# Emptying both banks of a matmul pair first: one change to a two-layer diffusion trunk on one core

## The chip, the cores and the metric

The kernel runs on one core of one Trainium2 chip. The metric is the device time of one execution in microseconds (us). The core has five engines with a queue each: TensorE (PE, with its weight loads as PEld), VectorE (DVE), ScalarE (ACT), GpSimd (POOL) and SyncE (SP), which issues nearly all DMAs. Each queue is worked off in order.

## The reference

One inference step of a backbone with two layers over 128 context tokens and 512 latent tokens, width 2048, float32. T is 640, the tokens of both groups together.

```python
for l in range(DEPTH):                                   # DEPTH = 2
    shift, scale, gate = modulation(c, ada_w[l], ada_b[l])    # c_ctx for the context tokens
    h = rms_norm(x, norm_g[l]) * (1.0 + scale) + shift
    if l % 2 == 0:   # windowed attention || gated linear attention
        y, side = even_mixer(h, w_in_even, ...)          # (concat of both) * silu(gate columns)
    else:            # neighbourhood attention || chunked spatial-gating MLP
        y, side = odd_mixer(h, w_in_odd, ...)            # (concat of both) * silu(gate columns)
    x = x + gate * (y @ w_out[l])
y = rms_norm(x, final_norm_g)
```

Nearly all the work is the products with `w_in_even`, `w_in_odd` and `w_out`. The products are taken at float32 accuracy from three float32r products (high x high, high x low, low x high).

## The kernel before

**Layout.** Activations lie feature-major: 16 k-tiles of 128 features x 640 tokens, split into a high and a low part (`acth`, `actl`, in the code `ah`, `al`). Two columns ahead of the tokens carry the modulation's shift, so that the projection of the shift comes out of the same matmuls. A chunk is 128 output features; it fills two PSUM banks of 320 tokens each (`pa`, `pb`). Weights are loaded to `wraw` or `rs`, ACT copies the high part to `whi`, and POOL or DVE subtracts it to leave the low part, `wlo`.

**Chunks and pairs.** Single chunks run in `chunk`, most of both output projections and of layer 1 in `spair`, a Strassen-like product over two chunks that uses folded sums of k-tiles (`eh`, `el`). Where one projection ends and the next begins, two chunks run together in `kpair`, k-tile by k-tile: a pair that frees k-tiles one by one is followed by a pair that takes the rewritten ones one by one. `STEPS` and `LAST` are the orders of the k-tiles, `skew` lets the second chunk lag the first by two steps. There are three such junctions: layer 0's last two gate chunks before the first output projection; that projection's last two chunks before layer 1's first v chunks; layer 1's last two gate chunks before the second output projection. `handover` starts the tasks of a junction: `loader` brings k-tiles from DRAM into free slots, `rewrite` (ACT and DVE or POOL) splits them into `acth` and `actl` as the old ones come free and raises `y0:k`, `x1:k` or `y1:k`, and two `fold` tasks build the folded sums, spill the second halves of six k-tiles to DRAM (`bh_dram`, `bl_dram`) and then refold them in place.

**Evacuation.** When a chunk is done its closure `evac(pa, pb)` is called. For a gate chunk (`gate`) it multiplies each half by `rstd`, adds the shift's projection (`bc`) inside a Silu, and multiplies the result `g` into y, half after half. For an output chunk (`out_evac`) it computes `x + G * psum`, squares it and adds the square to `ssq`, half after half; the x tile was loaded by the chunk's `pre`, called at the pair's start. `rstd1` turns `ssq` into layer 1's `rstd`.

**Order.** The emitted order of all instructions is fixed ahead by a planner written in the kernel: `Pace` keeps a model time for each engine and each range of a tile; `self.now` is PE's. Between matmuls `tick` advances the tasks in the list `self.tasks`, in order of the list, and the weight splits (`wpump`). A task yields a delay or waits for flags (`wait`), for data (`until`) or for an engine's queue to be short (`calm`); `need` lets the plan's time pass until a flag is up. Every vector, scalar and GpSimd instruction carries line 214, the matmuls of the projections 397, every SP load 431; groups are told apart by their tiles.

Of the kernel before, what the change touches and what calls it, by code (L numbers as in the profile page):

```python
# [239 lines left out]
class Trunk:  # L240
# [122 lines left out]
    def arena(self, slots):  # L363

        pool = self.tc.tile_pool(name=f"ar{self.n}", bufs=1)
        self.n += 1
        self.ar_pool = pool
        p = pool.__enter__()
        self.ar = self.t(p, [128, int(slots * T)], "arena")
        self.ar_at = 0  # L370
# [423 lines left out]
    def kpair(self, c1, c2, order, ready=None, free=None):  # L794

        for c in (c1, c2):
            if self.chunks[c][3]:
                self.chunks[c][3]()
        banks = {}
        self.quiet = True  # L800
        steps = self.skew(c1, c2, order)
        for i, (c, k) in enumerate(steps):
# [12 lines left out]
            if k == order[-1]:  # L815
                self.chunks[c][4](*banks[c])
                self.drop(*banks[c])
                self.flags.add(f"evac{c}")
        self.quiet = False

    def hpair(self, c1, c2, after):
# [150 lines left out]
    def handover(self, ready, free, used, order, at, src, loads, spare, cs, shift=None):  # L972
# [68 lines left out]
        def fold(w):  # L1041
# [30 lines left out]
            for i in range(w, NS, 2):  # L1072
                j, m = pairs[i]
                yield from self.wait(f"{used}:{j}")
                h, l = (x[:, j, CW:] for x in (self.ah, self.al))
                nc.vector.tensor_tensor(q, f32(self.ah[:, m, CW:]), f32(self.al[:, m, CW:]), ALU.add)
                sub(q, q, f32(h))
                sub(q, q, f32(l))
                yield from split(h, l, q)
                yield  # L1080
# [69 lines left out]
    def gate(self, y, ring):  # L1150
        nc = self.nc
        box = {}

        def evac(pa, pb):
            if pa is not None:
                bc = box["bc"] = self.s("bc", 2)
# [44 lines left out]

    def ssq_add(self, ssq, x, k, sq, c=slice(0, T), eng=None):
        nc = self.nc
        if k == 0:
            nc.scalar.activation(ssq[:, c], x[:, c], AF.Square)
        else:
            sq = sq[:, : c.stop - c.start]
            nc.scalar.activation(sq, x[:, c], AF.Square)
            (eng or nc.gpsimd).tensor_tensor(ssq[:, c], ssq[:, c], sq, ALU.add)

# [720 lines left out]
    def out_evac(self, l, n, f, xsrc, spill):  # L1931
# [3 lines left out]
        def square(y, c):  # L1935
            if l == 1 and f == KT - 1:
                nc.scalar.activation(self.sq[:, : c.stop - c.start], y[:, c], AF.Square)
            else:
                eng = nc.vector if l == 0 and n >= KT - 2 else nc.gpsimd
                self.ssq_add(self.ssq, y, f, self.sq if self.cut == CUT else self.sqs.next(), c, eng)  # L1940

        def evac(pa, pb):
            G, at = self.G[l], self.cut
            y = self.Y[:, n % NY, :]
            if pa is not None:
# [8 lines left out]
                )  # L1954
                square(y, slice(0, at))
            if pb is not None:
# [3 lines left out]
                )  # L1960
                square(y, slice(at, T))
                if l == 0 or n < NY:
                    self.dma(spill[:, f, :], y)

        def pre():
# [148 lines left out]
    def program(self):  # L2114
# [121 lines left out]
        def gate_chunk(w, y, pre=(), ring="gz", begin=None, then=None):  # L2236
            box = {}

            def evac(pa, pb):
                if "f" not in box:  # L2240
                    self.need(*pre)
                    box["f"] = self.gate(y() if callable(y) else y, L[ring])
                box["f"](pa, pb)
                if pb is not None and then:
                    then()

            add(w, 128, True, begin, evac)


        def open_att():  # L2250
            self.need("gla_done3")
            self.rp.__exit__(None, None, None)
            self.close_arena()
            self.arena(18.5)
            L["hq"], L["gx"] = self.take(T, 3), self.take(T, 2)
            L["hk"] = Ring([Y[:, 6, :], self.take()])
# [158 lines left out]

        do(lambda: self.spawn(rstd1(co)))
        do(lambda: self.spawn(last_gate()))
# [4 lines left out]
        for ct in range(8):  # L2422
# [11 lines left out]
            pre = (f"gv{ct - 4}",) if ct > 3 else ("r10", "r11")  # L2434
            add(wO[32 + ct], 128, True, None, lazy("vr", pre=pre, then=vdone, slots="DER"))
            if ct == 1:
# [363 lines left out]
```

## Time and profile before

| what | value |
|---|---|
| median of 3 runs | 2108.09 us (2107.87 to 2108.88) |
| profiled execution, its own time | 2113.52 us |
| its span | 2111.7 us |
| mean granted TensorE clock | 0.994 |
| PE, DVE, ACT, POOL busy | 2056.5, 1304.9, 1079.9, 1297.6 us |

The span is that of one profiled execution, 5.4 us over the median with what lies around it. In the views a row of a timeline has its start, its length, engine, line, operation, `out<-in` by the program's tile names, shapes and count; the bracket tells the idle time before it on that engine and what ended it. The row of a window has the stretch, its length, the busy time of PE, PEld, DVE, ACT and POOL with counts, the granted clock, the DMA engines' share and GB/s. `arena` holds working tiles (the slots A to E and R, gate products, x tiles), `adas` three more slots, `Y` the mixer's output.

The junctions lie, in that span, at about 820 to 895, 1035 to 1095 and 1850 to 1905 us.

### The profile page before, as it was taken

To read this page: it belongs to the slowest core of one execution; us is meant where nothing else is said; L and a number is where in the kernel's file an instruction comes from. 1 tells how busy PE (TensorE), PEld (TensorE's weight loads), DVE (VectorE), ACT (ScalarE), POOL (GpSimd) and SP (SyncE) were. 2 spreads that over 40 slices of the span, in tenths; PEclk is the share of its full clock that TensorE was granted. 3 is DMA by queue.
4 is the path that set the end of the run, shared out by engine and by line. 5 is a ranking of instruction groups with operands and counts; after the bars stand their busy time and mean duration, and the time that the engine had idled before them with its cause. 6 is when DMAs were issued, how large, how long until landed. Compare 5 with 4: busy or idle time off the path is not lost. (4 is left out here: it accounts for less than half of the span.)

```text
span 2111.7 us, 40271 instructions
## 1 busy us (share of the span) xinstructions
PE 2056.5 (97%) x14345; PEld 2004.6 (95%) x14345; DVE 1304.9 (62%) x3034; ACT 1079.9 (51%) x2493; POOL 1297.6 (61%) x1090
## 2 busy tenths in 40 slices
PE   7999999999999999999999999999999999999997
PEld 6899999999999999999989999999999999999996
DVE  4746686676465664797376878787454544455334
ACT  5645565454566766544564444444444554454443
POOL 4656565355455554798654666655555577768884
PEclk9999999999999999999999999999999999999999
DMA  9966343335465544575633455444222344363426
GB/s 355 391 210 213 117 135 130 117 115 174 148 204 173 173 159 148 164 228 181 228 121 107 137 160 149 138 156 144 94 82 94 97 140 131 116 223 120 137 93 239
DMA packets 192840, 340.17 MB, mean 161 GB/s; under 512 B 20896, under 2 KB 70144, under 8 KB 192640
## 3 DMA queue, kind: packets, MB, share of 16 engines
q1 hardware_dynamic: 191296, 336.45, 48.4%
q8 instruction: 112, 1.84, 0.4%
q10 hardware_dynamic: 1344, 1.17, 0.2%
q14 instruction: 88, 0.72, 0.1%
HBM read 303.03 MB, written 31.88 MB: 159 GB/s over the span
## 5 line engine op out<-in xcount | busy, mean ns | idle before, releaser
L397 PE MATMUL bank<-acth,whi 128*128 128x320 f32 (+3 forms) x3320 | 1023.2, 319 | 14.5 <-ACT bc L214 4.5
L397 PE MATMUL bank<-actl,whi 128*128 128x320 f32 (+3 forms) x3320 | 994.9, 311 | 2.6 <-POOL actl L214 1.4
L397 PE MATMUL bank<-acth,wlo 128*128 128x320 f32 (+3 forms) x3320 | 995.0, 311 | 0.8 <-POOL wlo L214 0.8
L214 POOL TENSOR_TENSOR wlo<-wraw,whi 128x512 fp32r<-128x512 f32 (+1 forms) x446 | 566.4, 1281 | 403.2 <-ACT whi L214 310.7
L397 PEld LDWEIGHTS bank<-acth,whi 128*128 128x128 f32 (+1 forms) x3320 | 618.3, 189 | 24.4 <-ACT bc L214 6.0
L397 PEld LDWEIGHTS bank<-actl,whi 128*128 128x128 f32 (+1 forms) x3320 | 618.3, 189 | 5.3 <-POOL actl L214 2.0
L397 PEld LDWEIGHTS bank<-acth,wlo 128*128 128x128 f32 (+1 forms) x3320 | 618.6, 189 | 1.5 <-POOL wlo L214 1.4
L214 POOL TENSOR_TENSOR wlo<-rs,whi 128x384 fp32r<-128x384 f32 x370 | 406.3, 1116 | 183.0 <-ACT whi L214 142.8
L214 ACT ACTIVATE whi<-wraw 128x512 fp32r<-128x512 f32 (+1 forms) x456 | 261.1, 587 | 96.0 <-PE bank L397 63.7
L214 ACT ACTIVATE whi<-rs 128x384 fp32r<-128x384 f32 x370 | 183.2, 516 | 60.9 <-PE bank L397 53.7
L397 PE MATMUL bank<-eh,whi 128*128 128x322 f32 (+1 forms) x666 | 208.9, 314 | 0.0
L397 PE MATMUL bank<-eh,wlo 128*128 128x322 f32 (+1 forms) x666 | 206.4, 310 | 0.7 <-POOL wlo L214 0.6
L397 PE MATMUL bank<-el,whi 128*128 128x322 f32 (+1 forms) x666 | 206.7, 310 | 0.0
L214 POOL TENSOR_TENSOR prod<-adas,mixrow 128x512 f32<-128x512 f32 x94 | 123.1, 1319 | 84.2 <-ACT prod L214 58.6
L214 DVE TENSOR_TENSOR wraw<-rs 128x768 f32<-128x768 f32 x74 | 97.3, 1314 | 124.7 <-DMA rs<-w_odd 45.9
L214 DVE CUSTOM_DVE_ANT_0 adas<-adas,bank,partg 128x256 bf16<-128x256 f32 (+1 forms) x290 | 156.1, 538 | 11.9 <-DMA adas<-ada_g 4.7
L214 ACT ACTIVATE arena<-arena,bc 128x512 f32<-128x512 f32 (+4 forms) x211 | 106.4, 527 | 82.4 <-DVE arena L214 79.4
L397 PEld LDWEIGHTS bank<-eh,wlo 128*128 128x128 f32 x666 | 125.5, 189 | 1.2 <-POOL wlo L214 1.2
L397 PEld LDWEIGHTS bank<-el,whi 128*128 128x128 f32 x666 | 125.8, 189 | 0.0
L397 PEld LDWEIGHTS bank<-eh,whi 128*128 128x128 f32 x666 | 125.5, 188 | 0.1
L214 DVE TENSOR_TENSOR bank<-bank,sums 128x320 f32<-128x320 f32 (+1 forms) x148 | 70.9, 493 | 74.5 <-PE bank L397 58.2
L214 DVE CUSTOM_DVE_ANT_0 adas<-adas,bank,part 128x512 bf16<-128x512 f32 x142 | 105.6, 744 | 5.6 <-DMA adas<-ada 2.6
(217 smaller groups left out, 2459.0 us busy)
## 6 DMA issues: line engine op xcount, KB each, us to landing
wraw<-w_even SPq DMA_DIRECT2D x176, 256.0 KB, 3.4
adas<-ada_g SPq DMA_DIRECT2D x128, 256.0 KB, 3.6
adas<-ada SPq DMA_DIRECT2D x128, 256.0 KB, 3.7
rs<-w_odd SPq DMA_DIRECT2D x50, 384.0 KB, 3.2
wraw<-w_odd SPq DMA_DIRECT2D x74, 256.0 KB, 3.5
wraw<-w_out SPq DMA_DIRECT2D x60, 256.0 KB, 3.7
rs<-w_odd SPq DMA_DIRECT2D x50, 256.0 KB, 3.6
Y<-ada SPq DMA_DIRECT2D x24, 512.0 KB, 7.5
```

The source lines that it names most:

```text
L214: return f(*args, **kw)
L397: self.nc.tensor.matmul(out, lhsT, rhs, start=start, stop=stop, **kw)
```

## The change

- In `kpair`, for a pair that takes rewritten tiles, the `pre` of a chunk (its x load) becomes a task, `begin`, that waits for the flags of the pair before and for all of the junction's loads; the evacuation asks for it.
- An `evac` may return a generator with what is left to do; `kpair` spawns these as tasks after both chunks (`finish`), and the flag `evac{c}` is raised at their end.
- `gate` with both banks at hand empties both by DVE (multiply, copy of the two shift columns, multiply), then runs two Silus over 128 and 512 tokens, and leaves the product with y to the task, one instruction over 640 tokens.
- `out_evac` with both banks empties both, then issues the spill; the squares follow, for the last two chunks of layer 0 as the task `squares`, which waits for `x1:14` and for short queues on ACT and DVE.
- The refold in `fold` yields until the planner expects the spills of the two parts to have been read.
- The ring of layer 0's gate products `gx` becomes a tile of its own in the arena's pool.
- `rstd1` goes to the head of the task list, and the first two v chunks no longer wait for slots D, E and R.

```diff
@@ -365,7 +365,7 @@
         pool = self.tc.tile_pool(name=f"ar{self.n}", bufs=1)
         self.n += 1
         self.ar_pool = pool
-        p = pool.__enter__()
+        p = self.ar_pool_ = pool.__enter__()
         self.ar = self.t(p, [128, int(slots * T)], "arena")
         self.ar_at = 0
 
@@ -795,8 +795,11 @@
 
         for c in (c1, c2):
             if self.chunks[c][3]:
-                self.chunks[c][3]()
-        banks = {}
+                if ready:
+                    self.spawn(self.begin(c, self.finishing), first=True)
+                else:
+                    self.chunks[c][3]()
+        banks, todo = {}, []
         self.quiet = True
         steps = self.skew(c1, c2, order)
         for i, (c, k) in enumerate(steps):
@@ -813,10 +816,29 @@
                 self.flags.add(f"{free}:{k}")
             self.tick(3)
             if k == order[-1]:
-                self.chunks[c][4](*banks[c])
+                if ready and self.chunks[c][3]:
+                    self.need(f"begun{c}")
+                last = self.chunks[c][4](*banks[c])
                 self.drop(*banks[c])
-                self.flags.add(f"evac{c}")
+                if last is None:
+                    self.flags.add(f"evac{c}")
+                else:
+                    todo.append((c, last))
+        self.finishing = [f"evac{c}" for c, _ in todo]
+        for c, last in todo:
+            self.spawn(self.finish(c, last), first=True)
         self.quiet = False
+
+    def begin(self, c, flags):
+        yield from self.wait(*flags, "loaded")
+        self.chunks[c][3]()
+        self.flags.add(f"begun{c}")
+        yield
+
+    def finish(self, c, last):
+        yield from last
+        self.flags.add(f"evac{c}")
+        yield
 
     def hpair(self, c1, c2, after):
 
@@ -1073,6 +1095,9 @@
                 j, m = pairs[i]
                 yield from self.wait(f"{used}:{j}")
                 h, l = (x[:, j, CW:] for x in (self.ah, self.al))
+                for e, x in (("a", h), ("v", l)):
+                    while (t := self.pace.ready(e, [self.pace.span(x)], []) - self.now) > 0:
+                        yield t
                 nc.vector.tensor_tensor(q, f32(self.ah[:, m, CW:]), f32(self.al[:, m, CW:]), ALU.add)
                 sub(q, q, f32(h))
                 sub(q, q, f32(l))
@@ -1151,7 +1176,20 @@
         nc = self.nc
         box = {}
 
+        def late(g):
+            yield from self.until(g)
+            nc.vector.tensor_tensor(y, y, g, ALU.mult)
+
         def evac(pa, pb):
+            if pa is not None and pb is not None:
+                bc = self.s("bc", 2)
+                g = y if ring is None else ring.next()
+                nc.vector.tensor_tensor(g[:, 0:HT], pa[:, 2 : 2 + HT], self.rstd[:, 0:HT], ALU.mult)
+                nc.vector.tensor_copy(bc, pa[:, 0:2])
+                nc.vector.tensor_tensor(g[:, HT:T], pb[:, 0:HT], self.rstd[:, HT:T], ALU.mult)
+                self.act(g[:, 0:NCTX], g[:, 0:NCTX], AF.Silu, bias=bc[:, 0:1])
+                self.act(g[:, NCTX:T], g[:, NCTX:T], AF.Silu, bias=bc[:, 1:2])
+                return late(g) if ring else None
             if pa is not None:
                 bc = box["bc"] = self.s("bc", 2)
                 g = box["g"] = y if ring is None else ring.next()
@@ -1199,14 +1237,14 @@
         nc.vector.scalar_tensor_tensor(self.rstd[:, c], t[:, :HT], 1.5, self.rstd[:, c], ALU.add, ALU.mult)
         yield
 
-    def ssq_add(self, ssq, x, k, sq, c=slice(0, T), eng=None):
+    def ssq_add(self, ssq, x, k, sq, c=slice(0, T)):
         nc = self.nc
         if k == 0:
             nc.scalar.activation(ssq[:, c], x[:, c], AF.Square)
         else:
             sq = sq[:, : c.stop - c.start]
             nc.scalar.activation(sq, x[:, c], AF.Square)
-            (eng or nc.gpsimd).tensor_tensor(ssq[:, c], ssq[:, c], sq, ALU.add)
+            nc.gpsimd.tensor_tensor(ssq[:, c], ssq[:, c], sq, ALU.add)
 
 
     def act_mod(self, l, k, x, t0, t1):
@@ -1936,8 +1974,20 @@
             if l == 1 and f == KT - 1:
                 nc.scalar.activation(self.sq[:, : c.stop - c.start], y[:, c], AF.Square)
             else:
-                eng = nc.vector if l == 0 and n >= KT - 2 else nc.gpsimd
-                self.ssq_add(self.ssq, y, f, self.sq if self.cut == CUT else self.sqs.next(), c, eng)
+                self.ssq_add(self.ssq, y, f, self.sq if self.cut == CUT else self.sqs.next(), c)
+
+        def squares(y):
+            if n == KT - 1:
+                yield from self.wait("squares")
+            for q, s in ((slice(0, HT), self.sqs.next()), (slice(HT, T), self.sqs.next())):
+                yield from self.wait("x1:14")
+                yield from self.calm(2.0, "a")
+                nc.scalar.activation(s, y[:, q], AF.Square)
+                yield from self.until(s)
+                yield from self.calm(4.0, "v")
+                nc.vector.tensor_tensor(self.ssq[:, q], self.ssq[:, q], s, ALU.add)
+                yield
+            self.flags.add("squares")
 
         def evac(pa, pb):
             G, at = self.G[l], self.cut
@@ -1952,15 +2002,20 @@
                 nc.vector.scalar_tensor_tensor(
                     y[:, NCTX:at], pa[:, NCTX:at], G[:, f, 1:2], x[:, NCTX:at], ALU.mult, ALU.add
                 )
-                square(y, slice(0, at))
+                if pb is None:
+                    square(y, slice(0, at))
             if pb is not None:
                 x = box["x"]
                 nc.vector.scalar_tensor_tensor(
                     y[:, at:T], pb[:, 0 : T - at], G[:, f, 1:2], x[:, at:T], ALU.mult, ALU.add
                 )
-                square(y, slice(at, T))
                 if l == 0 or n < NY:
                     self.dma(spill[:, f, :], y)
+                if l == 0 and n >= KT - 2:
+                    return squares(y)
+                if pa is not None:
+                    square(y, slice(0, at))
+                square(y, slice(at, T))
 
         def pre():
             x = box["x"] = self.xr.next()
@@ -2240,9 +2295,11 @@
                 if "f" not in box:
                     self.need(*pre)
                     box["f"] = self.gate(y() if callable(y) else y, L[ring])
-                box["f"](pa, pb)
+                last = box["f"](pa, pb)
                 if pb is not None and then:
+                    assert last is None
                     then()
+                return last
 
             add(w, 128, True, begin, evac)
 
@@ -2251,8 +2308,9 @@
             self.need("gla_done3")
             self.rp.__exit__(None, None, None)
             self.close_arena()
-            self.arena(18.5)
-            L["hq"], L["gx"] = self.take(T, 3), self.take(T, 2)
+            self.arena(16.5)
+            gx = self.t(self.ar_pool_, [128, 2 * T], "gx2")
+            L["hq"], L["gx"] = self.take(T, 3), Ring([gx[:, 0:T], gx[:, T : 2 * T]])
             L["hk"] = Ring([Y[:, 6, :], self.take()])
             L["av"] = self.take()
             L["vtoks"] = Ring([Y[:, 7, :], self.take()])
@@ -2413,7 +2471,7 @@
             self.low = [self.now, self.ada_task([job])]
             yield
 
-        do(lambda: self.spawn(rstd1(co)))
+        do(lambda: self.spawn(rstd1(co), first=True))
         do(lambda: self.spawn(last_gate()))
         acts.append(k)
         do(lambda: self.need("shift1"))
@@ -2432,7 +2490,7 @@
                     self.spawn(self.gmlp(Y.rearrange("p a b -> p (a b)")))
 
             pre = (f"gv{ct - 4}",) if ct > 3 else ("r10", "r11")
-            add(wO[32 + ct], 128, True, None, lazy("vr", pre=pre, then=vdone, slots="DER"))
+            add(wO[32 + ct], 128, True, None, lazy("vr", pre=pre, then=vdone, slots="DER" if ct > 1 else ""))
             if ct == 1:
                 pair("k", STEPS, "x1", None)
             elif ct == 3:
```

## The prediction

> **What bounds the kernel now.** I read the page first, then who makes TensorE wait, then the windows around those places, then the timeline there. The page:
>
> ```profile
> span 2111.7 us, 40271 instructions
> PE 2056.5 (97%) x14345; PEld 2004.6 (95%) x14345; DVE 1304.9 (62%) x3034; ACT 1079.9 (51%) x2493; POOL 1297.6 (61%) x1090
> ```
>
> TensorE (PE) sets the time; no other engine is over 62% busy. The change adds and removes no matmul, so it can win only PE's idle time and reduced clock where it acts. The PE waits between 835 and 1100 us (total, times, longest), and the busy time by stage:
>
> ```profile
> PE bank L397 <- DVE Y L214: 3.1, 2, 2.2
> PE bank L397 <- DVE arena L214: 2.1, 1, 2.1
> PE bank L397 <- POOL actl L214: 1.1, 1, 1.1
> PE bank L397 <- POOL wlo L214: 1.0, 2, 0.6
> PE bank L397 <- ACT bc L214: 0.9, 1, 0.9
> PE bank L397 <- ACT acth L214: 0.9, 1, 0.9
> ```
>
> ```profile
> 790.00:846.00 56.00, 56.00 (x376) 54.74 (x375) 26.13 (x67) 34.11 (x78) 23.14 (x18) 1.00 0.46 152
> 846.00:895.00 49.00, 45.41 (x294) 44.43 (x294) 39.74 (x69) 26.61 (x58) 36.09 (x27) 0.97 0.50 166
> 895.00:980.00 85.00, 84.62 (x577) 84.36 (x576) 78.38 (x180) 35.45 (x80) 73.95 (x69) 1.00 0.69 222
> 1060.00:1095.00 35.00, 29.90 (x183) 28.53 (x182) 27.71 (x49) 24.30 (x50) 21.75 (x16) 0.95 0.28 97
> 1870.00:1930.00 60.00, 59.02 (x396) 58.08 (x395) 44.26 (x84) 33.70 (x75) 47.45 (x38) 1.00 0.40 134
> ```
>
> Columns are the stretch, its length, busy PE, PEld, DVE, ACT, POOL, then PE's clock. The edited places lose 3.59 us (846 to 895, behind the layer-0 gate pair), 0.38 (895 to 980), 5.10 (1060 to 1095, behind the last pair of the first output projection) and 0.98 (1870 to 1930, behind the layer-1 gate pair). Sum 10.05 us. One matmul takes 84.62/577 = 0.147 us.
>
> The clock adds to it:
>
> ```profile
> 846.40:849.80 3.40, 0.86 (x5) 0.37 (x3) 1.27 (x2) 1.72 (x5) 2.81 (x2) 1.00 0.46 177
> 849.80:853.20 3.40, 2.93 (x11) 2.94 (x12) 1.75 (x5) 2.11 (x5) 1.55 (x1) 0.50 0.21 54
> 1061.50:1064.90 3.40, 2.15 (x15) 1.87 (x13) 2.67 (x4) 2.17 (x5) 3.40 (x3) 1.00 0.04 15
> 1085.40:1088.80 3.40, 1.43 (x8) 0.91 (x7) 3.05 (x9) 3.04 (x7) 1.85 (x2) 0.99 0.43 145
> 1088.80:1092.20 3.40, 3.40 (x14) 3.40 (x14) 2.73 (x5) 3.17 (x7) 1.99 (x2) 0.50 0.18 61
> ```
>
> Behind a stretch with 2.54 us idle (3.40 - 0.86), and behind one with 1.97, PE runs 3.40 us at clock 0.50, a loss of 1.7 us each; behind one with 1.25 idle it keeps 1.00. All that the change can reach is therefore 10.05 + 3.4 = 13.4 us.
>
> **The change part by part.** *A, gate pair before the first output projection (846 to 895).*
>
> ```profile
> 844.08 0.49 DVE L214 TENSOR_TENSOR arena<-bank,rstd 128x320 f32<-128x320 f32 x1 [4.54 <-PE bank L397]
> 847.57 0.15 ACT L214 ACTIVATE bc<-bank 128x2 f32<-128x2 f32 x1
> 847.78 0.41 PE L397 MATMUL bank<-acth,whi 128*128 128x320 f32 x1 [0.93 <-ACT bc L214]
> 848.53 1.28 DVE L214 TENSOR_TENSOR Y<-Y,arena 128x320 f32<-128x320 f32 x1 [3.96 <-ACT arena L214]
> 849.73 0.48 DVE L214 TENSOR_TENSOR arena<-bank,rstd 128x320 f32<-128x320 f32 x1
> 850.27 0.64 PE L397 MATMUL bank<-acth,whi 128*128 128x320 f32 x1 [2.08 <-DVE arena L214]
> 851.36 3.93 SPq L431 DMA_DIRECT2D arena<-xT  x2
> 877.34 1.13 DVE L214 SCALAR_TENSOR_TENSOR Y<-bank,G,arena 128x128 f32<-128x128 f32 x3 [2.39 <-issue]
> ```
>
> The first bank is multiplied at 844.08, but its two shift columns are copied by ACT only at 847.57, and the second bank comes behind the gate product (848.53, 1.28) on DVE. PE waits 0.93, then 2.08. After the change DVE does multiply, copy, multiply from 844.08: 0.49 + c + 0.48. The trace has no such copy on DVE; c lies between ACT's 0.15 and a whole 128x320 pass, 0.49. I take 0.15, the row of the same size. Both banks are then free at 845.2 (at latest 845.5), and PE comes at 846.85 (847.78 - 0.93): 3.0 us go, and the half clock behind them, 1.7. One Silu fewer per chunk is off the path.
>
> The x loads move behind the product task. They now land for the evacuation at 877.34; issued at 851.36, they have 26 us, so a few microseconds later they cost nothing. On SP they no longer stand in front of weight loads. Waiting behind the new wait are only those two loads; the first evacuation of the next pair asks for them. If that cover went, an evacuation and with it two banks would be late.
>
> Late next is the rewrite of the activations for the next pair:
>
> ```profile
> 865.05 1.57 POOL L214 TENSOR_TENSOR actl<-Y,acth 128x640 fp32r<-128x640 f32 x1
> ```
>
> The tile with this low part (index 3) is used at step 20 of the pair, 6 matmuls of 0.147 each: 846.85 + 20 x 0.88 = 864.5, against 866.6. If no rewrite moved, 2.1 us would come back; but ACT, which was held until 847.57 and again by DVE, is freed earlier. I take 0.7 (0 to 2.1). A: -4.7 + 0.7 = -4.0.
>
> *B, last pair of the first output projection (1060 to 1095).*
>
> ```profile
> 1062.45 0.66 DVE L214 SCALAR_TENSOR_TENSOR Y<-bank,G,arena 128x128 f32<-128x128 f32 x2
> 1063.84 1.47 DVE L214 TENSOR_TENSOR arena<-arena 128x320 f32<-128x320 f32 x1 [0.73 <-ACT arena L214]
> 1065.24 0.54 DVE L214 SCALAR_TENSOR_TENSOR Y<-bank,G,arena 128x320 f32<-128x320 f32 x1
> 1070.27 0.49 DVE L214 TENSOR_TENSOR arena<-arena 128x320 f32<-128x320 f32 x1 [0.60 <-ACT arena L214]
> 1065.83 0.42 PE L397 MATMUL bank<-acth,whi 128*128 128x320 f32 x1 [2.19 <-DVE Y L214]
> 1062.64 0.74 ACT L214 ACTIVATE acth<-adas 128x640 fp32r<-128x640 f32 x1
> 1072.21 0.74 ACT L214 ACTIVATE acth<-adas 128x640 fp32r<-128x640 f32 x1
> 1086.14 0.74 ACT L214 ACTIVATE acth<-Y 128x640 fp32r<-128x640 f32 x1
> 1086.93 0.56 PE L397 MATMUL bank<-acth,whi 128*128 128x322 f32 x2 [0.90 <-ACT acth L214]
> 1088.56 0.74 PE L397 MATMUL bank<-actl,whi 128*128 128x322 f32 x2 [1.06 <-POOL actl L214]
> ```
>
> The square's sum (1063.84) stands between the emptying of one bank and the other. With the squares as tasks, the three reads run 0.66 + 0.54 from 1062.45 to 1063.65, where PE arrives (1065.83 - 2.19 = 1063.64). Of the 3.1 us behind "DVE Y" 0.1 stays: -3.0.
>
> B2 is the wait at 1086.93 and 1088.56: 1.96 idle and 1.7 of clock. Here PE waits for a rewritten tile, and it now comes 3.0 earlier, so the rewrite must be 5.0 earlier for the wait to go. Between 1062.64 and 1072.21 not one tile is rewritten: 9.6 us in which DVE and ACT alternate on squares. The squares now give way to the rewrite of tile 14 (they wait for "x1:14") and to short queues. Four more tiles follow it, the last from 1086.14 on, so one per 13.9/4 = 3.5; a gap of 3.5 in place of 9.6 puts the rewrite 6.1 ahead. Bounds: 6.1 clears the wait (-3.7); none gives B back (+3.0). I take the gain with 1 us of wait and part of a half-clock stretch left, nearer the first since the gap's cause is removed: -2.0.
>
> *C, gate pair before the second output projection.* Of 0.98 us idle the bank wait goes, a rewrite wait stays: -0.4 (-1.0 to +0.5).
>
> *Refold waits.*
>
> ```profile
> 883.02 0.44 ACT L214 ACTIVATE acth<-bank 128x320 fp32r<-128x320 f32 x1 [1.81 <-DMA bh_dram<-acth]
> 893.93 0.41 PE L397 MATMUL bank<-eh,wlo 128*128 128x320 f32 x1 [0.59 <-POOL wlo L214]
> ```
>
> ACT stands 1.81 us at a spill, with weight copies queued behind it; PE waits 0.59 for a weight's low part ten microseconds later. The task now yields instead: -0.2 (-0.6 to 0). Against it, PE enters the stage from 895 four microseconds earlier, where DVE is busy 78.4 of 85 and POOL 74.0: +1.0 (0 to 4.0, all of A).
>
> *Gate ring, release check, rstd first.*
>
> ```profile
> 823.05 1.75 SPq L431 DMA_DIRECT2D arena<-yT_dram  x4
> ```
>
> The ring's own tile bears on these four loads. PE is busy 56.00 of 56.00 us until 846, so their being earlier or later within that cover is 0. The release check dropped for two v chunks and rstd's place show no PE wait: 0. In the first pair of each projection the squares only swap order: 0.
>
> Sum: -4.0 - 3.0 - 2.0 - 0.4 - 0.2 + 1.0 = -8.6. The profiled execution took 2113.52, 5.4 over the median of 2108.09; the difference carries over: 2108.1 - 8.6 = **2099.5 us**.
>
> **The rivals.** *Given back:* PE merely meets each rewrite sooner. For: DVE is busy 27.7 of 35 in B, and both next waits are rewrites. Against: the 9.6 us hole. B and B2 cancel, A leaves 4.7 - 2.1 = 2.6: 2105.5.
>
> *Slower: the sums come too late.* The rewrites of tiles 6 and 7 wait for the last pair's "evac" flags, now set only after its four squares, taken in turn behind two queue checks each; rstd follows those flags too. Tile 6 is needed near step 26, 1063.6 + 26 x 0.88 = 1086.5. Squares done later than about 1083 (one rewrite of 3.5 us before) stall PE by as much, and half clock adds 1.7. If they end at 1094, PE loses 11 + 1.7, B2's 2.0 is lost as well: -8.6 + 14.7 = +6: 2114. For: waiting tasks have no due time. Against: four squares inline ended at 1070.8 (the row at 1070.27), which leaves 12 us.
>
> *The clock stays.* The half clock has another cause than the gaps: A wins 3.0 less 0.7, B2 keeps 1.7 of clock of which I count half won: 2108.1 - 8.6 + 1.7 + 0.85 = 2102. Against: both half-clock stretches sit right behind the idlest ones. [...]
>
> **How the numbers follow.** Forecast 0.62, given back 0.18, slower 0.16, clock stays 0.04. Single runs spread by 1 us; 0.2% is 4.2 us, about what a measurement can tell. Faster by over that: 0.62 + 0.04 = 0.66; within: 0.18; slower: 0.16. The range runs from nearly all 13.4 us won, 2095.0, over "given back" to no change and a bit, 2109.5; the slower case is left out.
>
> **What would show it.** Right: no PE wait on "bc", "DVE arena" or "DVE Y" behind a pair; clock 1.00 from 846 to 1095; rewrites of tiles in every 4 us between 1062 and 1072. Given back: the waits reappear under "acth" or "actl" in the same pairs. Slower: rstd or tiles 6 and 7 as releasers near 1087. Wrong beyond all these: new waits in stages that the change does not name, since the emitted order is planned and shifts everywhere.

## The result

| kernel | median (range, runs) | ratio to before, 95% interval |
|---|---|---|
| before | 2108.95 us (2106.23 to 2113.98, 8) | 1 |
| the change | 2102.70 us (2098.91 to 2108.36, 8) | 0.9967 [0.9952, 0.9982] |
| the change, measured again | 2102.61 us (2101.91 to 2107.02, 9), before 2109.22 | 0.9969 [0.9960, 0.9979] |

The change gains 6.3 us (2108.95 - 2102.70). The forecast was 2099.5, a gain of 8.6 over its 2108.1. The profiled execution of the changed kernel took 2104.64 us. The page:

```profile
span 2102.8 us, 40256 instructions
PE 2052.0 (98%) x14345; PEld 2000.7 (95%) x14345; DVE 1305.9 (62%) x3034; ACT 1078.3 (51%) x2485; POOL 1301.4 (62%) x1090
```

Busy PE fell by 4.5 us with the same 14,345 matmuls, mostly because fewer matmuls run at half clock, where they last longer: in before 14 lie in 3.40 us at clock 0.50 (1088.80 to 1092.20) and 25 at 0.99 (853.20 to 856.60). Ahead of its end, before's profile has five stretches of 3.41 us at clock 0.50 (from 61.35, 115.97, 119.38, 849.83 and 1088.77 us on), this one two (from 61.15 and 115.77 us on). One of the three that went is that from 119.38 us on, where both kernels still issue the same instructions; only the two at the junctions are the change's work. What makes PE wait between 835 and 1100 us (total, times, longest):

```profile
PE bank L397 <- POOL wlo L214: 3.7, 5, 1.0
PE bank L397 <- ACT eh L214: 0.9, 1, 0.9
```

All waits of before on "DVE Y", "DVE arena", "POOL actl", "ACT bc" and "ACT acth" are gone. The waits on POOL's weight parts (`wlo`) grew from 1.0 to 3.7 us. The windows that answer to those of before, moved by what PE had won by then:

```profile
844.50:889.80 45.30, 43.31 (x289) 42.38 (x289) 35.49 (x63) 25.16 (x53) 35.73 (x27) 1.00 0.50 166
889.80:979.20 89.40, 86.59 (x582) 85.08 (x580) 78.86 (x183) 34.47 (x79) 73.26 (x69) 1.00 0.66 213
1059.00:1086.30 27.30, 27.30 (x183) 26.98 (x182) 21.25 (x36) 19.17 (x38) 18.70 (x13) 1.00 0.32 105
1860.60:1921.40 60.80, 59.65 (x402) 58.89 (x401) 49.01 (x84) 33.40 (x72) 47.75 (x37) 1.00 0.38 129
```

Behind the output projection's last pair PE is busy in 27.30 of 27.30 us, at full clock; before it lost 5.10 us there. Behind the layer-0 gate pair 1.99 us idle remain, and the next window, where before lost 0.38, now loses 2.81.

Both kernels issue the same 14,345 matmuls, up to about 1070 us in the same order and behind that with a few small ones of `rstd1` at other places, so their starts can be set against each other one by one. The offset between the two executions steps where time is won or lost. The two profiles of the change agree (places are in the time of before, here and in all steps named below):

| place (us of before) | forecast | step, first profile | step, second profile |
|---|---|---|---|
| A, gate pair, 847.8 | -4.7 | -3.50 | -3.07 |
| rewrite, refold, stage after A, 857 to 973 | +0.7 - 0.2 + 1.0 | +4.21 | +4.33 |
| B, last output pair, 1065.8 and 1076.7 | -3.0 | -4.24 | -4.03 |
| B2, 1086.9 to 1101.6 | -2.0 | -3.33 | -3.33 |
| C, 1881 to 1922 | -0.4 | -0.25 | -0.23 |
| sum from 780 us on | -8.6 | -7.1 | -6.3 |

Ahead of 780 us the offsets differ from profile to profile, from -7.4 to +0.2, most of it ahead of 220 us, where all kernels issue the same instructions; the places below are therefore compared from 780 us on, and totals by medians.

What stands at A after the change (timeline):

```profile
842.60 0.49 DVE L214 TENSOR_TENSOR arena<-bank,rstd 128x320 f32<-128x320 f32 x1 [4.89 <-PE bank L397]
843.01 0.15 DVE L214 COPY bc<-bank 128x2 f32<-128x2 f32 x1
843.08 0.48 DVE L214 TENSOR_TENSOR arena<-bank,rstd 128x320 f32<-128x320 f32 x1
846.06 0.49 DVE L214 TENSOR_TENSOR el<-bank,eh 128x320 fp32r<-128x320 f32 x1 [2.50 <-ACT eh L214]
...
848.25 0.48 DVE L214 TENSOR_TENSOR arena<-bank,rstd 128x320 f32<-128x320 f32 x1
848.66 0.15 DVE L214 COPY bc<-bank 128x2 f32<-128x2 f32 x1
848.72 0.48 DVE L214 TENSOR_TENSOR arena<-bank,rstd 128x320 f32<-128x320 f32 x1
...
848.95 0.72 PE L397 MATMUL bank<-acth,whi 128*128 128x320 f32 x2 [0.91 <-ACT eh L214]
```

The first chunk is emptied as forecast: multiply, copy (0.15, as assumed), multiply, from 842.60, before the next pair begins at 845.2. The second chunk is done at about 845.2 too, but DVE, which works its queue in order, stands 2.50 us at an instruction of a fold (`el`, which wants ACT's `eh`) and empties the chunk from 848.25 on. PE waits 0.91. The row names ACT's `eh` as what ended that wait, at 848.82; DVE's copy from the second chunk's bank (848.66 and 0.15) ended within 0.01 us of it, and PE's queue stands at a semaphore for DVE just ahead, for 0.05 us from 848.85 on, so the bank is what PE needed.

### The profile page after: what moved, and what is told of

Its sections match the earlier page's. It is cut to its first block, busy times and chain, and to the rows that moved or that the text cites. A ratio compares the mean times of both kernels' runs of the same rounds, so it can differ in the third digit from the quotient of the medians.

```text
span 2102.8 us, 40256 instructions
## 1 busy us (share of the span) xinstructions
PE 2052.0 (98%) x14345; PEld 2000.7 (95%) x14345; DVE 1305.9 (62%) x3034; ACT 1078.3 (51%) x2485; POOL 1301.4 (62%) x1090
## 4 chain that ended last, share of the span: by engine, by line
PE 79%; DMA 7%; DVE 6%; POOL 3%; issue 3%; ACT 2%; SPq 1%; ACTq 0%; POOLq 0%; DVEq 0%
PE bank L397 76%; POOL wlo L214 2%; PE bank L402 2%; DVE arena L214 1%; DVE adas L214 1%; DVE Y L214 1%; DMA adas<-gateT 1%; DMA more<-ada 1%; DVE bank L214 1%; ACT arena L214 1%; DMA Y<-xT 1%; DMA adas<-ada 1%; SPq L431 1%; PE bank L1426 1%; POOL actl L214 0%
## 5 line engine op out<-in xcount | busy, mean ns | idle before, releaser
L214 ACT ACTIVATE arena<-arena,bc 128x512 f32<-128x512 f32 (+4 forms) x189 | 97.8, 538 | 76.4 <-DVE arena L214 71.3
```

The lines of the kernel that those rows point to most:

```text
L214: return f(*args, **kw)
```

## The experiments

Each kernel is the change with one edit, unless said otherwise. Times are medians, ratios those to before, run beside them (its medians were 2108.98 for e1 to e4, 2109.38 for e5 to e8 and 2109.22 for e9 to e11); "from 780" is the sum of the steps from 780 us on against before, as in the table above.

| label | median | ratio, interval | from 780 |
|---|---|---|---|
| e1_gate_old | 2108.47 | 0.9998 [0.9989, 1.0007] | +0.5 |
| e2_squares_inline | 2103.72 | 0.9976 [0.9966, 0.9985] | -5.7 |
| e3_gate_only | 2111.81 | 1.0015 [1.0002, 1.0027] | +3.2 |
| e4_less_filler | 2101.30 | 0.9967 [0.9955, 0.9979] | -7.9 |
| e5_ring_in_arena | 2099.59 | 0.9957 [0.9942, 0.9973] | -9.1 |
| e6_refold_old | 2110.55 | 1.0005 [0.9992, 1.0017] | +0.1 |
| e7_square_tasks | 2103.10 | 0.9972 [0.9961, 0.9983] | -5.0 |
| e8_out_evac_old | 2107.75 | 0.9996 [0.9987, 1.0006] | -0.6 |
| e9_arena_and_tasks | 2096.70 | 0.9942 [0.9930, 0.9954] | -12.5 |
| e10_arena_less_filler | 2099.52 | 0.9952 [0.9939, 0.9964] | -9.6 |
| e11_ring_again | 2097.71 | 0.9947 [0.9933, 0.9961] | -9.9 |

### Is A what wins at the gate pair, and does early arrival cost the rest? (e1)

```diff
-            if pa is not None and pb is not None:      # gate's evac: empty both first
+            if False:                                  # half after half, as before
```

> The changed kernel with the gate chunks evacuated half after half as before; all else changed. After the layer-0 gate pair the changed kernel is 3.5 us ahead of the kernel before, and between 857 and 972 us it loses 4.2 us again in waits for weight low parts (POOL wlo). Theory 'early': those waits are there because TensorE enters the Strassen stage sooner than ACT, DVE and POOL can serve it; with the old evacuation TensorE is late again, the 3.7 us of wlo waits fall below 1, and the time is within 1 us of the changed kernel, about 2103. Theory 'order': the planner has merely put the instructions of that stage in a worse order; the waits stay, the 3.5 us are lost on top: about 2106.

Measured: 2108.47, so without the gate edit nothing of the change is left in the time. That is more than either theory lost: against before, e1 loses 1.9 us at A, where the change wins 3.5, and 2.3 at C. PE's waits between 835 and 975 us, and three stretches of 3.40 us:

```profile
PE bank L397 <- DVE arena L214: 2.7, 1, 2.7
PE bank L397 <- POOL wlo L214: 2.2, 4, 0.9
PE bank L397 <- ACT bc L214: 1.2, 1, 1.2
```

```profile
844.00:847.40 3.40, 1.03 (x6) 0.54 (x4) 0.78 (x1) 2.50 (x6) 3.40 (x4) 1.00 0.00 1
847.40:850.80 3.40, 1.88 (x7) 1.88 (x8) 2.37 (x4) 0.90 (x3) 2.25 (x2) 0.50 0.24 77
850.80:854.20 3.40, 3.40 (x15) 3.40 (x14) 2.16 (x6) 1.77 (x4) 0.59 (x1) 0.50 0.33 96
```

The waits on `bc` and `arena` are back, with the half clock behind them, this time for two stretches. The `wlo` waits fall from 3.7 to 2.2 us, not below 1, although PE comes late, and of the 4.2 us lost between 857 and 973 2.9 are still lost. PE's coming early is therefore at most a part of that loss; the rest lies in the order in which the instructions now stand.

### The gate edit alone, and the refold wait (e3, e6)

e3 is before with the hunks of `kpair`, `gate` and the gate chunk; e6 is the change without the wait of the refold:

```diff
-                for e, x in (("a", h), ("v", l)):
-                    while (t := self.pace.ready(e, [self.pace.span(x)], []) - self.now) > 0:
-                        yield t
```

> The kernel before with the new gate evacuation, its product task and the x-load task alone. Theory 'early': 3.5 us won after the layer-0 gate pair, nearly all lost again in wlo waits before 975: 2108 to 2109, as before. Theory 'order': 3.5 us won and kept: about 2105.4. The layer-1 gate pair adds a gain of 0 to 1 us in both.

> The changed kernel whose refold no longer yields until the spills have been read. Theory 'pair': once the gate pair is emptied early, ACT stands at the spill for longer (4.45 us with the gate evacuation alone, which then cost TensorE a 2.8 us wait and half clock near 885); so this edit is what keeps the gain, and without it 4 to 6 us are lost: 2107 to 2109. Forecast's size: 0.2 us, 2102.9. Rival for the later wlo waits: this edit put the stage's order wrong; then wlo waits fall from 3.7 to below 1 here.

Measured: 2111.81 (ratio 1.0015, just slower than before) and 2110.55 (1.0005); the change is 8 to 9 us faster than both. In both A is won (-4.85 and -3.55 at 847.8) and lost again behind 887 (+5.25 and +7.59). Timeline and windows of e6:

```profile
881.27 0.44 ACT L214 ACTIVATE acth<-bank 128x320 fp32r<-128x320 f32 x1 [4.04 <-DMA bh_dram<-acth]
882.17 0.63 PE L397 MATMUL bank<-acth,whi 128*128 128x320 f32 x1 [4.32 <-ACT whi L214]
```

```profile
878.20:881.60 3.40, 0.00 (x0) 0.00 (x0) 3.30 (x7) 0.33 (x1) 0.00 (x0) 1.00 1.00 360
881.60:885.00 3.40, 2.65 (x8) 2.25 (x9) 3.13 (x7) 2.01 (x7) 2.81 (x3) 0.50 0.81 272
885.00:888.40 3.40, 3.40 (x14) 3.40 (x14) 3.36 (x6) 1.50 (x5) 2.30 (x3) 0.50 0.00 1
```

ACT stands 4.04 us at the refold's write, which must wait until the spill has read the tile; the copies of the weights (`whi`) are queued behind it, PE waits 4.32 for one of them and then runs two stretches at half clock. In e3, where only the gate edit is added to before, the same row stands 4.45 us; before had 1.81. In the change no such row of ACT is left. So the gate edit is worth nothing without the refold wait, and the wait keeps what the edit wins: taking out the gate edit costs the change 5.8 us (e1), taking out the refold wait 7.9 (e6). What the wait is worth alone, added to before, was not run. The expectation of e6 also had a rival, that the wait is what makes `wlo` late behind it: those waits fall to 2.0 us here, not below 1, and PE comes later too, so this is not settled.

### The output evacuation, whole and in parts (e8, e2)

e8 puts `out_evac` back as it was. e2 keeps "both banks first", but leaves the last two chunks' squares in line behind it, their sums on DVE:

```diff
-                if l == 0 and n >= KT - 2:
-                    return squares(y)
```

> The changed kernel with the output chunks evacuated and squared half after half as before, rstd still first. With squares in line but both banks emptied first the gain stayed whole (3.75 us at 1066 and 2.75 at 1087), so the order of emptying is what counts: here both are lost, 7 us with the clock: 2109 to 2110. Rival: the second gain comes from elsewhere (rstd's place, the release check): then only 3.75 are lost, 2106.5.

> The changed kernel with the squares of layer 0's last two chunks not as a task but in line, behind the emptying of both banks. Theory 'hole': the tasks matter because squares in line keep the rewrite of the next k-tiles waiting; the bank wait (DVE Y, 3.1 us) stays gone, but the wait for tile 3 near 1081 to 1088 comes back with half clock, 3.7 us: about 2106.4. Rival 'banks only': emptying both banks first is all that counts, the second wait does not come back: about 2102.7. If the squares of the first chunk also delay the emptying of the second, a bank wait of about 1 us is seen.

Measured: 2107.75 and 2103.72. PE's waits between 1040 and 1100 us, in e8 and then in e2:

```profile
PE bank L397 <- DVE Y L214: 3.2, 2, 2.2
PE bank L397 <- POOL actl L214: 1.0, 1, 1.0
PE bank L397 <- POOL wlo L214: 0.5, 1, 0.5
```

```profile
PE bank L397 <- POOL actl L214: 1.0, 1, 1.0
```

e8 has B's wait back whole, 3.2 us under "DVE Y"; e2 wins it (-3.75 at 1065.8). B is thus what emptying both banks first wins. B2 is not. At 1086.9 e8 wins 2.7 us like e2 (2.75), of the change's 3.76; it loses 1.0 at 1081, ahead of that. The wait under "ACT acth" and the half clock behind it stay away, although ACT again has 9.6 us without a rewrite. ACT's rewrites on both sides of that hole in e8, and PE at B2:

```profile
1061.23 0.74 ACT L214 ACTIVATE acth<-adas 128x640 fp32r<-128x640 f32 x1
1070.80 0.74 ACT L214 ACTIVATE acth<-adas 128x640 fp32r<-128x640 f32 x1
```

```profile
1084.20:1087.61 3.41, 2.42 (x17) 2.15 (x16) 1.89 (x5) 3.38 (x8) 2.31 (x2) 1.00 0.09 34
1087.61:1091.02 3.41, 3.41 (x26) 3.41 (x25) 3.31 (x7) 2.71 (x7) 2.85 (x3) 1.00 0.43 132
```

The rival of e8's expectation, that this gain comes from elsewhere, holds for 2.7 us. e1, e5 and e6 keep it too, so none of the gate edit, the ring's tile and the refold wait is needed for it; and the x-load task with the gate edit does not bring it, for e3 still waits 0.5 us under "ACT acth" and 1.1 under "POOL actl". `rstd1`'s place and the v chunks' dropped wait for slots stand in e1, e2, e5, e6 and e8 and were not taken out; what brings the 2.7 us stays open. That the squares are tasks is worth the 1.0 us that stays under "POOL actl" in e2, and about 1 us in the median, within its spread.

### The ring's own tile (e5, e11)

```diff
-            self.arena(16.5)
-            gx = self.t(self.ar_pool_, [128, 2 * T], "gx2")
-            L["hq"], L["gx"] = self.take(T, 3), Ring([gx[:, 0:T], gx[:, T : 2 * T]])
+            self.arena(18.5)
+            L["hq"], L["gx"] = self.take(T, 3), self.take(T, 2)
```

> The changed kernel with the gate ring gx back in the arena. Theory 'forecast': the ring's own tile is worth nothing, 2102.7, since TensorE has no wait at that place. Rival: the ring's own tile shifts the plan of loads and folds, which alone brings the gain behind the gate pair (3.5 us) or the loss in wlo waits (4.2 us): then 2106 or 2099, and the waits between 845 and 975 differ by that much.

> The change with the gate ring back in the arena, again, now beside the change itself on one chip. If the ring's own tile costs time, it is 1.5 to 3.5 us faster than the change; if the difference between the two earlier results was spread, the two agree within 1 us.

> The change as it is, beside the three others on one chip: 2102.7 within 1 us.

The last two ran on one chip: 2097.71 (2096.29 to 2099.73) against 2102.61 (2101.91 to 2107.02). The ranges do not meet; the medians differ by 4.9 us, those of the earlier results by 3.1. From 780 us on the first pair of profiles shows 2.0 of it (-9.1 and -7.1) and the second 3.6. What lies ahead of that cannot be put down to the ring: there both kernels issue the same instructions but for one small pair of ACT's at 500 us, and the second pair of profiles differs in the mean clock, 0.994 in the change and 0.996 in e11. The ring's own tile thus costs the change 2.0 to 3.6 us by the traces; the rest of the 4.9 stays open. DVE at the gate pair with the ring in the arena (e11), and then SP's loads of the output-projection's tiles in the change and in e11:

```profile
836.76 0.49 DVE L214 TENSOR_TENSOR arena<-bank,rstd 128x320 f32<-128x320 f32 x1 [4.64 <-PE bank L397]
...
839.42 0.49 DVE L214 TENSOR_TENSOR arena<-bank,rstd 128x320 f32<-128x320 f32 x1 [1.71 <-PE bank L397]
...
842.18 1.39 DVE L214 TENSOR_TENSOR Y<-Y,arena 128x640 f32<-128x640 f32 x1 [1.81 <-ACT arena L214]
...
847.71 0.49 DVE L214 TENSOR_TENSOR el<-bank,eh 128x320 fp32r<-128x320 f32 x1 [0.51 <-ACT eh L214]
```

```profile
835.63 0.37 SPq L431 DMA_DIRECT2D arena<-yT_dram  x1
...
839.26 0.42 SPq L431 DMA_DIRECT2D arena<-yT_dram  x1
```

```profile
832.25 0.38 SPq L431 DMA_DIRECT2D arena<-yT_dram  x1
...
834.88 0.58 SPq L431 DMA_DIRECT2D arena<-yT_dram  x1
```

In e11 the second chunk is emptied as soon as PE is done with it (839.42, released by "PE bank"), and the folds' `el` comes behind both gate products, 847.71. In the change the loads are issued 9.6 to 5.9 us ahead of the next pair's start at 845.2, in e11 7.2 to 4.5 ahead of 839.4: with its own tile for the ring these y tiles come earlier, and the folds stand in front of the second chunk's evacuation; that the one brings the other is read from the order and was not tried by itself. Without it A wins -4.70 (e5) and -4.81 (e11), the forecast's -4.7, in place of -3.50 and -3.07; and the `wlo` waits fall from 3.7 and 3.8 to 3.0 and 2.7. Why the loads move with the ring's place was not tried.

### What the stage after A loses (e7, e9, e4, e10)

Timeline of the change, where `wlo` is late:

```profile
906.86 0.93 ACT L214 ACTIVATE arena<-Y 128x320 f32<-128x320 f32 x2 [5.49 <-DVE Y L214]
907.41 2.43 POOL L214 TENSOR_TENSOR arena<-arena 128x320 f32<-128x320 f32 x2 [3.59 <-ACT arena L214]
909.80 2.69 POOL L214 TENSOR_TENSOR wlo<-wraw,whi 128x384 fp32r<-128x384 f32 x2
```

ACT stands 5.49 us at a chunk's square (`arena<-Y`), which waits for DVE's evacuation; POOL stands 3.59 us at the sum of that square, and the weight parts are queued behind both. e7 makes the squares of layer 0 from its third chunk on into tasks that wait for the data and for short queues; e9 does so for chunks 2 to 9 only, with the ring in the arena. e4 and e10 leave less room on DVE for the modulation's filler work (0.3 in place of 1.5), without and with the ring in the arena:

```diff
+                if l or n < 2 or n >= KT - 6:           # e9; e7: if l or n < 2
+                    return self.ssq_add(...)
+                def work():
+                    yield from self.until(y[:, c])
+                    yield from self.calm(2.0, "ag")
+                    self.ssq_add(self.ssq, y, f, self.sqs.next(), c)
+                    yield
+                self.spawn(work())
```

> The changed kernel in which the squares of layer 0's output chunks in the Strassen stage are tasks too: ACT takes a square only when the plan has its input ready and ACT and POOL have short queues. Theory: the wlo waits come from ACT standing up to 5.5 us at a square whose input DVE has not yet written, with weight copies queued behind it; then ACT's waits for 'DVE Y' go and the wlo waits fall from 3.7 to below 1: 2099.5. Rival: DVE or POOL itself is short; the waits stay, 2102.7.

> The change with the gate ring back in the arena, and in the first output projection the squares of chunks 2 to 9 as tasks that wait for short queues (the last chunks ahead of the hand-over keep theirs in line). Theory 1, that an ACT queue standing at squares delays the weight copies and so wlo, and that the ring's own tile costs a little: wlo waits between 857 and 972 fall from 3.0 us to 1.5 or less, no half clock near 1055, and the time is 1 to 3 us below the ring in the arena alone, about 2097.5. Theory 2, that the planner's filler takes back what one place gains: wlo waits fall, but as much waits elsewhere, 2099.6 within 1 us.

> The changed kernel with the modulation's products (background work on DVE) let in only when DVE's planned queue is 0.3 us ahead of TensorE instead of 1.5, from the first output projection on. Theory: DVE is kept full by this background work, so sums and evacuations of the Strassen stage come late, ACT's squares and POOL's adds queue behind them, and weight low parts are late; then the 3.7 us of wlo waits fall below 1 and the time is about 2099.5. Rival: the waits do not come from that work: 2102.7, no change. If the modulation of layer 1 is then finished too late, a stall near 1030 us shows: 2105 or more.

> The change with the gate ring back in the arena and less room for filler tasks (0.3 in place of 1.5). If the two single results add up (the ring in the arena about 2 us, less filler about 1 us), 2098; if less filler's effect was only that a plan moved, 2099.6 within 1.5 us either way.

e7 gains nothing, 2103.10. Between 857 and 973 it loses nearly nothing (-0.1 in place of +4.2), but near 1058 it loses 4.21, 1.7 of it clock, and wins back 3.96 behind it, so that B's 4.24 is gone; 2.02 more go at 2076. Its waits from 1040 to 1100 us and the two stretches:

```profile
PE bank L397 <- POOL wlo L214: 1.3, 1, 1.3
PE bank L397 <- ACT whi L214: 1.0, 1, 1.0
```

```profile
1051.60:1055.01 3.41, 1.36 (x8) 0.83 (x6) 3.25 (x8) 3.18 (x7) 2.36 (x2) 1.00 0.00 0
1055.01:1058.42 3.41, 3.17 (x12) 3.17 (x13) 1.83 (x5) 1.75 (x5) 3.34 (x3) 0.50 0.25 80
```

The squares put off meet the next junction's rewrites. e9 stops them ahead of it. Its waits from 850 to 975:

```profile
PE bank L397 <- POOL wlo L214: 0.8, 2, 0.5
PE bank L397 <- ACT whi L214: 0.3, 1, 0.3
```

From 1040 to 1100 it has none. A keeps -4.85, nothing net is lost between 857 and 973 (+0.2), B and B2 are as in the change, and from 780 us on it stands at -12.5. With the squares out of the line the late `wlo` goes, in e7 and in e9. Why the change loses there what before did not is another question, for in before the squares stand in line too. ACT's and POOL's idle time at squares and PE's waits for `wlo` over this stage (us in total, times, longest), by the views of waits:

| kernel, stretch | ACT `arena` <- DVE Y | POOL `arena` <- ACT | PE <- POOL `wlo` |
|---|---|---|---|
| before, 857 to 974 | 34.7, 11, 5.4 | 8.8, 6, 3.9 | 1.0, 2, 0.6 |
| the change, 852 to 973 | 37.0, 9, 6.1 | 17.6, 8, 4.8 | 3.7, 5, 1.0 |
| e9, 850 to 967 | 7.9, 5, 2.1 | 1.1, 1, 1.1 | 0.8, 2, 0.5 |

ACT stands at squares about as long in before; what doubled is POOL's standing at their sums. Which part of the change doubled it stays open. In time e9 is the fastest of all, 2096.70, 12.5 us below before (0.9942 [0.9930, 0.9954]) and 5.9 below the change on the same chip; against e11's 2097.71 the intervals overlap, so the tasks' own gain of 1 us is not settled.

Less filler does not add: e10 is not faster than e11 (2099.52 and 2097.71). In e10 the steps from 857 to 973 fall to +1.2, but +1.5 appears at 993 to 1000, where e11 has none. e4 against the change is inconclusive in time (the same ratio, 0.9967); its steps from 857 to 973 fall to +1.5, its `wlo` waits to 2.2 us and not below 1, and +0.9 appears at 974 to 1040.

## Why the prediction was right, and where it was off

The direction and the range (2095.0 to 2109.5) held, and so did the mechanism at A's first chunk and at B; the median lies 3.2 us above the forecast. That the sum came so near is in part luck: the stage after A lost 2.7 us more than forecast for its three terms and A won 1.2 less, while B and B2 won 2.6 more between them, B2 for a reason that was not the forecast's.

**A** was forecast at -4.7 at the wait itself and gave -3.50 and -3.07. The copy's 0.15, the half clock and the first chunk's early emptying are as worked out. The step that failed is "Both banks are then free": it looked at the first chunk alone and did not ask what is emitted on DVE between the two evacuations. With the ring in the arena, where nothing is, A gives -4.70 and -4.81.

**The ring's own tile** was put at 0, since the y loads lay beside full PE. It costs 2.0 to 3.6 us from 780 us on, with no load that is late. The four loads that the forecast showed do not move: they go out 23.6 us ahead of the next pair in the change and 23.7 in e11. The four behind them do, and they lie beside full PE as well; that being earlier "within that cover is 0" was the wrong bound, since what follows a load in its consumers' queues can move ahead with it, as the folds' `el` stands ahead of the second chunk's evacuation in the change (846.06 and 848.25) and behind it in e11 (847.71 and 839.42).

**Rewrite after A** was put at +0.7. No wait on `acth` or `actl` is left between 835 and 1100 us: 0.

**Refold waits** were put at -0.2 by ACT's 1.81 us at the spill in the trace of before. That was the price at PE's old time. With A won, ACT stands there 4.45 us (e3) and 4.04 (e6), and in e6 that costs PE 7.59. The term was coupled with A and sized as if A did not happen; the gain that it keeps was already counted in A, so the sum was not harmed.

**The stage from 895** was put at +1.0 within 0 to 4.0, for PE's coming early. From 857 to 973 4.2 and 4.3 went, nearly all behind 893; "all of A" as the upper bound was just passed. The reason given carries a part at most: in e1 PE comes late and 2.9 are lost all the same. The loss runs through the squares ahead of the weight copies, for without them in line it goes (e7, e9); why it is larger than in before stays open.

**B** was forecast at -3.0 and gave -3.75 at 1065.8 and -0.49 at 1076.7. **B2** was -2.0 and gave -3.33 net, near its full bound of -3.7. The hole in the rewrites is gone, as forecast, but that is not what won B2. ACT's rewrites in the change, and then two that follow each other in e2:

```profile
1062.78 0.74 ACT L214 ACTIVATE acth<-adas 128x640 fp32r<-128x640 f32 x1
1065.34 0.74 ACT L214 ACTIVATE acth<-adas 128x640 fp32r<-128x640 f32 x1
1067.02 0.74 ACT L214 ACTIVATE acth<-Y 128x640 fp32r<-128x640 f32 x1
1070.16 0.74 ACT L214 ACTIVATE acth<-Y 128x640 fp32r<-128x640 f32 x1 [1.51 <-DVE Y L214]
```

```profile
1068.09 0.74 ACT L214 ACTIVATE acth<-Y 128x640 fp32r<-128x640 f32 x1
1074.60 0.74 ACT L214 ACTIVATE acth<-Y 128x640 fp32r<-128x640 f32 x1
```

Here tiles are rewritten every 1.7 to 3.1 us where before had 9.6 without one. In e2, with the squares in line, 6.5 us pass without one (1068.09 to 1074.60), and B2 still gives -2.75. In e8 the whole hole is back, and 2.7 us at 1086.9 are won all the same. The step that failed is "the gap's cause is removed" as the reason for the gain: squares in line account for 1.0 us of wait, emptying both banks first for none of the 2.7, and these come with some other part of the change; the two edits that no run takes out, `rstd1`'s place and the release check, the forecast put at 0. That B2's size came out near its bound is luck.

**C** was -0.4 and gives about nothing, -0.25 by the steps and +0.1 by the offset at 1880 and at 1926: the waits under "DVE arena" and "POOL actl" go (-1.73), and a `wlo` wait of 1.1 comes at 1922 (+1.48).

**The rivals.** "Given back" happened to A and not to B, and not under `acth` or `actl` as described. "The sums come too late" did not happen. "The clock stays" named 2102, near the result, and still did not happen: the gaps went and the clock is 1.00 at both places, while e1, with the gaps at A back, has the half clock back too:

```profile
847.40:850.80 3.40, 2.49 (x16) 2.11 (x15) 3.35 (x7) 3.17 (x7) 3.40 (x3) 1.00 0.21 77
1081.40:1084.80 3.40, 3.40 (x24) 3.31 (x23) 2.41 (x4) 0.82 (x3) 1.31 (x1) 1.00 0.03 5
```

## What to carry to other kernels

Price each part of a change at the times that the other parts make: a stall of 1.81 us cost PE at most 0.59 before, and one of 4.04 at the same place cost 7.6 once PE came 3.5 us earlier. Where a queue is worked in order, an operation that has nothing to do with the path still cost where it was emitted ahead of an evacuation or a weight copy before its data were there (DVE's 2.50 us at `el`, PE 0.91; ACT's 4.04 at the refold in e6, PE 4.32); look for standing rows ("4.04 <-DMA", "5.49 <-DVE") on ACT, DVE and POOL, and put off the work behind them, but not into the next hand-over. A load that goes out earlier need not be free where its followers move forward with it: with the ring's own tile the y loads go out earlier and 2.0 to 3.6 us are lost. And take out each part of a change by itself before a gain is put down to it: B2 was won without the hole that seemed to explain it being closed.

## What was not expected of the hardware

At the junctions of before, e1 and e7 the half clock came behind stretches in which PE still worked. In the traces of before and of the change, apart from the end of an execution, it holds for one stretch of 3.41 us or for two (before, 115.97 to 122.79). At the junctions it followed stretches with 2.54 and 1.97 us idle (before), 2.05 (e7: 3.41 - 1.36) and 2.37 (e1), and lasted two where the next stretch had 1.52 idle as well (e1) or the first had no matmul at all (e6). It did not follow stretches with 1.25 idle (before) or 0.91 (the change). No single wait of PE at the junctions of before, e1 and e7 was longer than 2.7 us.

The idle time of one stretch did not settle it alone. In before the stretch 112.55 to 115.97 has 1.65 us idle, and the next one has clock 0.50; the stretch 180.82 to 184.23 has 1.64 idle, and the next one has clock 1.00:

```profile
112.55:115.97 3.42, 1.77 (x24) 1.42 (x24) 1.29 (x4) 0.28 (x1) 1.27 (x1) 1.00 0.88 321
115.97:119.38 3.41, 2.81 (x24) 2.39 (x24) 0.70 (x2) 1.98 (x5) 0.15 (x1) 0.50 0.46 159
180.82:184.23 3.41, 1.77 (x12) 1.51 (x12) 0.58 (x1) 1.90 (x5) 1.18 (x1) 1.00 0.83 253
184.23:187.65 3.42, 3.42 (x25) 3.42 (x25) 2.38 (x8) 2.50 (x6) 1.31 (x2) 1.00 0.83 250
```

At B in before the gap of 2.19 us falls into two stretches, with 1.22 and 0.96 us idle in all, and the clock stays at 1.00:

```profile
1061.46:1064.87 3.41, 2.19 (x15) 1.91 (x13) 2.68 (x4) 2.21 (x5) 3.41 (x3) 1.00 0.04 14
1064.87:1068.28 3.41, 2.45 (x16) 2.45 (x17) 2.64 (x6) 1.06 (x3) 0.10 (x1) 1.00 0.44 164
1068.28:1071.70 3.42, 2.47 (x16) 2.16 (x15) 2.24 (x5) 2.34 (x6) 0.87 (x1) 1.00 0.56 182
```

What decides between these cases stays open.
